# One block of the modulation sums moved from the key projection to the output projection

## The chip, the cores and the metric

The kernel runs on one core of one Trainium2 chip. A core has a matrix engine (TensorE, "PE" in the profile, its weight loads "PEld"), a vector engine (VectorE, "DVE"), a scalar engine (ScalarE, "ACT"), a general engine (GpSimd, "POOL") and a queue that issues the transfers (SyncE, "SP"). Each works through its own list of instructions in a fixed order and waits on semaphores for the others. The metric is the time of one execution on the device, in microseconds (us).

## The reference

One layer of a streaming encoder, for a sequence of 512 tokens and a width of 2048, all in float32:

```python
mod = c @ w_ada[l] + b_ada[l]
sh1, sc1, g1, sh2, sc2, g2 = [m[:, None, :] for m in jnp.split(mod, 6, axis=-1)]
h = x * (1.0 + sc1) + sh1
mix = token_mixer(h, ...)          # one input projection, three head groups, output projection w_o
x = layer_norm(ALPHA * x + g1 * mix, ln1_g[l], ln1_b[l])
h = x * (1.0 + sc2) + sh2
ff = jnp.square(jax.nn.relu(h @ w_ff1[l])) @ w_ff2[l]
x = layer_norm(ALPHA * x + g2 * ff, ln2_g[l], ln2_b[l])
```

The mixer projects h to the inputs of three groups: an S5 state-space scan with a gated linear unit, a gated convolution of width 3, and attention over 8 heads that keeps 128 keys per query, chosen by an indexer (scores, then a top-k mask). `c` is one vector, so `mod` is a product of a vector with a matrix of 2048 x 12288: some 100 MB of weights for very little arithmetic.

## The kernel before, in words

Matrix products run on TensorE in three passes: each weight tile is loaded as float32 (tile `raw`), split into a rounded part (`wh`, ScalarE, line 57) and the rest (`wl`, VectorE, line 60), and multiplied (lines 196 to 198 or 208 to 210). A quad is four k-tiles of 128 rows and 512 columns, 1 MB; `w_quads` loads one, steps the background queue, and splits it in two halves. `raw` has four buffers, which all loads of this kind share.

The modulation sums don't use TensorE for the product. `ada_acc` loads 1 MB (two rows of tiles of 128 x 1024) and adds each with VectorE to a running sum, weighted by an element of c per partition: `adaz <- raw * c + adaz` (line 63; the first of a block is a plain product, line 67, unless the sum starts from a bias row, when GpSimd clears the tile, line 220, and a small load, line 222, puts the bias into one row). A block is 1024 columns: 8 loads, 16 VectorE operations. Then a sink adds up over the partitions with small matmuls: `to_cols` (line 254) into a column of `mod2`, `to_rows` (line 246) into tiles `g1` that hold a gate for all rows. There is one buffer for `adaz`, so a block's first operation waits for the sink of the block before.

These blocks are generators in a list `bg`. `tick()` takes one step of the first of them: a load and its two sums; when a block is used up, the same step runs its sink and goes on to the first load of the next. `pump_tick()` is called once per quad and makes as many steps as `pump[0]` says, with fractions carried over. So `PUMP` sets how many loads go beside a quad of each stage.

The order of the stages in the program, with the quads of each: the first projections (indexer, query) in four groups of k-tiles; keys (8 quads), S5 (no quads), values (8 quads, rate 0), attention (none), convolution (three weight groups of 4 quads), output projection (16 quads in four column blocks `nb`), LayerNorm with the second modulation, MLP. The compiler's scheduler gives each engine its list: it takes the instruction of highest priority that is ready by its own estimate, in program order where priorities are equal. `prio(name)` raises it by an entry of `PRIO`: in the stages up to the convolution a weight split has 1000, a modulation sum 300, attention 600, S5 300, top-k 60, the indexer -100; in the output projection a split has 1500, its evictions 5000, a sum 150, and the loads of weights and sums 1500 each. The sinks' matmuls have none, so they keep their place among the program's matmuls.

Eight blocks belong to this change's surroundings: two for the gate g1 (`g1_jobs`) and four for the second shift and scale (`mod_jobs`: shift, scale, shift, scale, half of the width each). Two more, for the gate g2, come in the MLP and stay as they are. In the kernel before, three of `mod_jobs` are queued ahead of the keys; 16 steps there take the first two, the convolution's 12 steps take the third, and the output projection's 24 steps (1.5 per quad) and a few forced ones take gate block one, the fourth, gate block two. At the end of a column block the gate must be there: `while len(g1s) <= nb: tick()` forces steps until it is. After the projection four small operations finish `mod2`, and LayerNorm applies it while it transposes each row tile (`hf`).

Of the kernel before, what the change touches and what calls it, by code (L numbers as in the profile page):

```python
# [25 lines left out]
            wo=5000, ln1=150, ff1=3000, ff2=4000, hc=300, hc_load=300, tx=2000, ln2=150, index=-100, topk=60, rope=600, ssm0=600, ssm=300, glu=150,  # L26
            w_load0=4000, w_load1=300, w_load2=1500, w_load3=2500, w_split0=5000, w_split1=1000, w_split2=1500,
            w_split3=4000, ada_load0=4000, ada_load1=4000, ada_load2=1500, ada_load3=2500, ada0=5000, ada1=300,
            ada2=150, ada3=300)
PUMP = dict(start=0, keys=2, values=0, conv=1, wo=1.5)  # L30
BIG = 1e30
TWO_PI = 2.0 * math.pi
PI_LO = float(np.nextafter(np.float32(math.pi), np.float32(0)))
# [18 lines left out]
def trunk_kernel(ctx, tc, A, out):  # L52
# [3 lines left out]
    def act(o, i, f=AF.Copy, **kw):  # L56
        S.activation(o, i, f, **kw)  # L57

    def tt(o, a, b, op):
        V.tensor_tensor(o, a, b, op=op)  # L60

    def stt(o, a, s, b, op0, op1):
        V.scalar_tensor_tensor(o, a, s, b, op0=op0, op1=op1)  # L63
# [17 lines left out]
    def prio(name):  # L81
        if name not in PRIO:
            name += str(stage_no[0])
        return tc.high_priority(offset=PRIO[name])

    def bank(n="mm"):
        if "two" in pools:
            return two_banks()[:, 0]
        return pools[n].tile([128, 512], F32, name=n)
# [40 lines left out]
    def w_split(src, kk, n, pool=None, tag="w"):  # L130

        k2 = kk if pool else 2
        h = (pool or stage).tile([128, k2, n], F32R, name=tag + "h", bufs=3)[:, :kk]
        l = (pool or stage).tile([128, k2, n], F32R, name=tag + "l", bufs=3)[:, :kk]
        with prio("w_split"):
            split(h, l, src)
        return h, l

    def w_ks(dram, k0, k1, tick, pool, w=2):

        for a in range(k0, k1, w):
            b = min(a + w, k1)
            if w == 1:
                tick(a)
            r = load(dram[a:b].rearrange("k p n -> p k n"), [128, b - a, 512], pool, "rw")
            if w > 1:
                tick(b - a)
            h, l = w_split(r, b - a, 512)
            for j in range(a, b):
                yield j, h[:, j - a], l[:, j - a]  # L150

    bg = []

    def tick(n=1):

        for _ in range(n):
            while bg:
                try:
                    next(bg[0])
                    break  # L160
                except StopIteration:
                    bg.pop(0)

    pump, owed = [0], [0.0]
# [29 lines left out]
    def mm3(ps, wh, wl, xh, xl, start, stop):  # L194

        T.matmul(ps, wh, xh, start=start, stop=False)  # L196
        T.matmul(ps, wl, xh, start=False, stop=False)  # L197
        T.matmul(ps, wh, xl, start=False, stop=stop)  # L198
# [125 lines left out]
    def ensure(k):  # L324
        while ready[0] <= k:
            tick()
# [3 lines left out]
    mod_jobs = []  # L330
# [3 lines left out]
    for gi, (k0, k1) in enumerate(KGROUPS):  # L334
        n_ada = 2 * (KGROUPS[gi + 1][1] - KGROUPS[gi + 1][0]) if gi + 1 < len(KGROUPS) else PUMP["start"]
        n_w = 5 * (k1 - k0) - (k1 - k0 if gi == 0 else 0)
        done = [0, 0]

        def pace(n):
            done[0] += n  # L340
            want = min(-(-done[0] * n_ada // n_w), n_ada)
            tick(want - done[1])
            done[1] = want

        if gi > 0:
            ensure(k1 - 1)
        if gi == len(KGROUPS) - 1:
            bg.extend(mod_jobs[:3])

        first_k, last_k = k0, k1 - 1  # L350

        def evac_acc(dst, ps):
            with prio("kw"):
                if gi == 0:
                    act(dst, ps)
                else:
                    tt(dst, ps, dst, OP.add)


        banks = held[:2] + [bank() for _ in range(2)] + held[2:]  # L360
        if gi == 0:
            ws = w_ks(A["wA"], k0, k1, ensure, FP, 1)
        else:
            ws = w_ks(A["wA"], k0, k1, pace, FP)
        for k, h, l in ws:
            rb = FP.tile([128, 1, 80], F32, name="rkw")
            with prio("first"):
                nc.sync.dma_start(rb[:, 0], A["wkw"][k])
            hb, lb = w_split(rb, 1, 80, FP, "kw")
            for m in range(4):  # L370
                lim = (0, KT - 1) if m < 2 else (first_k, last_k)
                mm3(banks[m], h[:, m * 128:(m + 1) * 128], l[:, m * 128:(m + 1) * 128],
                    acts[:, k, 0], acts[:, k, 1], k == lim[0], k == lim[1])
            mm3(banks[4][:80], hb[:, 0], lb[:, 0], acts[:, k, 0], acts[:, k, 1], k == 0, k == KT - 1)
        for m in range(2, 4):
            evac_acc(u_t[:, m], banks[m])
        if last_k == KT - 1:
            with prio("kw"):
                act(kiwi[:80], held[2][:80])
                for m in range(2):  # L380
                    act(u_t[:, m], held[m])

        for b in range(2):
            banks = [bank() for _ in range(3)]
            for k, h, l in w_ks(A["wqi"][b], k0, k1, pace, FP):
                for t in range(3):
                    tk = slice((t + 1) * 128, (t + 2) * 128)
                    mm3n(banks[t], h, l, acts[:, k, 0, tk], acts[:, k, 1, tk], k == first_k, k == last_k)
            for t in range(3):
                evac_acc(qi_n[t][:, b * 512:(b + 1) * 512], banks[t])  # L390

        for b in range(2):
            banks = [bank() for _ in range(4)]
            for k, h, l in w_ks(A["wq"][b], k0, k1, pace, FP):
                for m in range(4):
                    mm3(banks[m], h[:, m * 128:(m + 1) * 128], l[:, m * 128:(m + 1) * 128],
                        acts[:, k, 0], acts[:, k, 1], k == first_k, k == last_k)
            for m in range(4):
                evac_acc(q_t[b][:, m], banks[m])
# [117 lines left out]
    def proj_t(dram, evac, quads=(0, 1, 2, 3), banks=None):  # L517
        banks = banks or [bank() for _ in range(4)]
        for i, (k, h, l) in enumerate(w_quads(dram, quads)):
            for m in range(4):  # L520
                mm3(banks[m], h[:, m * 128:(m + 1) * 128], l[:, m * 128:(m + 1) * 128],
                    acts[:, k, 0], acts[:, k, 1], i == 0, i == KT - 1)
        with prio("evac"):
            for m in range(4):
                evac(m, banks[m])
# [5 lines left out]

    pump[0] = PUMP["keys"]
    for b in range(2):
# [301 lines left out]
    VP = vp.enter_context(tc.tile_pool(name="vpool", bufs=3, reuse_waits="tile"))  # L835
    pump[0] = PUMP["values"]
    for b in range(2):
# [91 lines left out]

    pump[0] = PUMP["conv"]
    CV = mix.enter_context(tc.tile_pool(name="conv", bufs=1, reuse_waits="tile"))
    z_t = CV.tile([128, 4, SEQ], F32, name="z_t")
    proj_t(A["wconv"][0], lambda m, ps: act(z_t[:, m], ps))

    def conv_h(m, ps):
        tt(z_t[:, m], ps, z_t[:, m], OP.mult)
# [35 lines left out]
    wo = ExitStack()  # L974
# [4 lines left out]

    pump[0] = PUMP["wo"]  # L980
    stage_no[0] = 2
    g1_jobs = [ada_block(j, to_rows(g1_tile), True) for j in range(2)]
    bg.extend([g1_jobs[0], mod_jobs[3], g1_jobs[1]])
    xwh = WO.tile([128, 8, 512], F32R, name="xwh", bufs=1)
    xwl = WO.tile([128, 8, 512], F32R, name="xwl", bufs=1)
    for nb in range(4):
        banks = [bank() for _ in range(NT)]
        last = nb == 3

        def part(t, i, k, h, l):  # L990
            tk = slice(t * 128, (t + 1) * 128)
            mm3n(banks[t], h, l, acts[:, k, 0, tk], acts[:, k, 1, tk], i == 0, i == KT - 1)

        for i, w in enumerate(w_quads(A["wo"][nb], korder[:2] if last else korder)):
            for t in range(NT):
                part(t, i, *w)
        if last:
            ws = w_keep(A["wo"][nb], korder[2:], xwh, xwl)
            for t in range(NT):
                for i, w in enumerate(ws):  # L1000
                    part(t, 8 + i, *w)
        while len(g1s) <= nb:
            tick()
        for t in range(NT):
          with prio("wo"):
            o = r1[:, t, nb * 512:(nb + 1) * 512]
            xr = WO.tile([128, 512], F32, name="xr", bufs=2)
            nc.sync.dma_start(xr, A["x"][t * 128:(t + 1) * 128, nb * 512:(nb + 1) * 512])
            tt(o, banks[t], g1s[nb], OP.mult)
            stt(o, xr, ALPHA, o, OP.mult, OP.add)  # L1010
            V.bn_stats(out=stats[:, t, nb], in_=o)

    ts(mod2[:, 0], mod2[:, 0], 1.0, None, OP.add)
    tt(mod2[:, 3], mod2[:, 0], col("ln1b", 0, 16), OP.mult)
# [615 lines left out]
```

## Time and profile before

| | us |
|---|---|
| median of 3 runs | 2221.06 |
| range of the runs | 2219.15 to 2222.51 |
| the profiled execution: its time | 2218.12 |
| the profiled execution: its span, first to last instruction | 2216.3 |
| TensorE busy | 2138.7 (96%) |
| VectorE busy | 1878.6 (85%) |
| ScalarE busy | 1041.5 (47%) |
| sums into `adaz` (line 63), 180 operations | 198.2 |

Busy times are sums over the instructions of an engine; matmuls overlap in a pipeline, so a busy TensorE is not one at its peak. Idle time of an engine matters only where it is the one that the others wait for. Stretches are given in us from the first instruction; they follow the stages roughly: keys 250 to 340, values to 455, attention, S5 and convolution to 706, output projection to 877, LayerNorm to 925. The granted clock of TensorE is 0.993 of its full 2.4 GHz on the mean.

### The profile page before, as it was taken

The page shows a single profiled execution, that of the slowest core. Times are in us where ns is not written, and L with a number is a line of the kernel's source. Part 1 is how long each engine was busy: PE and PEld are TensorE (multiplying, and loading weights), DVE is VectorE, ACT ScalarE, POOL GpSimd, SP SyncE. Part 2 cuts the span into 40 slices and gives each one's busy share as a digit, 9 for nine tenths or more (in the row PEclk, how much of TensorE's full clock was granted, in tenths as well). Part 3 has the DMA queues.
Part 4 walks back from the last instruction along what each step waited for, and adds up shares of the span by engine and source line. Part 5 has one row for each costly group of instructions (what it writes and reads, how often), then busy time and mean ns, then how long its engine had stood idle before and what let it go on. Part 6 is the DMA issues. An engine that isn't in the chain of part 4 may idle for free.

```text
span 2216.3 us, 30985 instructions
## 1 busy us (share of the span) xinstructions
PE 2138.7 (96%) x12043; PEld 1845.9 (83%) x12043; DVE 1878.6 (85%) x2520; ACT 1041.5 (47%) x1394; POOL 44.6 (2%) x55
## 2 busy tenths in 40 slices
PE   6999999998999999989999999999899999999997
PEld 4778887876777787889999999999778887888886
DVE  7886799999867776798888888886789988998788
ACT  3423444344644313666666665665444444444432
POOL 0000000010000000000000000000000000000000
PEclk9999999999999999999999999999999999999999
DMA  8887653364334676756566556564888898798462
GB/s 326 316 305 280 200 216 135 107 235 164 103 119 157 243 277 255 241 172 229 182 205 203 188 198 206 181 209 141 301 295 275 280 318 280 245 341 275 134 218 86
DMA packets 198171, 489.80 MB, mean 221 GB/s; under 512 B 18052, under 2 KB 106500, under 8 KB 171656
## 3 DMA queue, kind: packets, MB, share of 16 engines
q1 hardware_dynamic: 191496, 475.24, 61.0%
q0 software_dynamic: 6528, 12.58, 3.1%
q8 instruction: 94, 1.54, 0.3%
q14 instruction: 53, 0.43, 0.1%
HBM read 394.45 MB, written 80.74 MB: 214 GB/s over the span
## 4 chain that ended last, share of the span: by engine, by line
PE 50%; issue 29%; DVE 14%; DMA 4%; ACT 3%; SPq 0%; POOL 0%; DVEq 0%; ACTq 0%; POOLq 0%
PE two L1396 7%; PE two L1397 7%; PE two L1395 7%; PE mm L209 4%; PE mm L197 4%; PE mm L210 4%; PE mm L208 3%; PE mm L198 3%; PE mm L196 3%; DVE wl L60 3%; DVE adaz L63 2%; PE two L210 1%; PE two L209 1%; PE two L208 1%; DVE x L60 1%
## 5 line engine op out<-in xcount | busy, mean ns | idle before, releaser
L57 ACT ACTIVATE wh<-raw 128x1024 fp32r<-128x1024 f32 x332 | 351.1, 1058 | 437.5 <-PE two L1397 140.8
L60 DVE TENSOR_TENSOR wl<-raw,wh 128x1024 fp32r<-128x1024 f32 x332 | 403.7, 1220 | 106.5 <-ACT wh L57 105.3
L1395 PE MATMUL two<-wh,hin 128*128 128x512 f32 x784 | 307.4, 392 | 5.7 <-ACT wh L57 5.0
L1396 PE MATMUL two<-wl,hin 128*128 128x512 f32 x784 | 306.5, 391 | 4.1 <-DVE wl L60 4.0
L1397 PE MATMUL two<-wh,hin 128*128 128x512 f32 x784 | 305.8, 390 | 0.0
L196 PE MATMUL mm<-acts,wh 128*128 128x512 f32 (+1 forms) x568 | 223.0, 396 | 5.7 <-ACT wh L57 3.3
L197 PE MATMUL mm<-acts,wl 128*128 128x512 f32 (+1 forms) x568 | 224.0, 394 | 1.7 <-DVE wl L60 1.5
L198 PE MATMUL mm<-acts,wh 128*128 128x512 f32 (+1 forms) x568 | 221.2, 391 | 0.0
L63 DVE SCALAR_TENSOR_TENSOR adaz<-raw,cols,adaz 128x1024 f32<-128x1024 f32 (+2 forms) x180 | 198.2, 1111 | 16.9 <-DMA raw<-in_adaR_dram 12.8
L202 PE MATMUL mm<-acts,wh 128*128 128x256 f32 x720 | 204.0, 283 | 3.1 <-ACT wh L57 2.4
L203 PE MATMUL mm<-acts,wl 128*128 128x256 f32 x720 | 203.8, 283 | 1.8 <-DVE wl L60 1.8
L203 PE MATMUL mm<-tx,wl 128*128 128x256 f32 x720 | 203.8, 283 | 1.1 <-DVE wl L60 1.1
L204 PE MATMUL mm<-acts,wh 128*128 128x256 f32 x720 | 203.7, 283 | 0.0
L204 PE MATMUL mm<-tx,wh 128*128 128x256 f32 x720 | 203.3, 282 | 0.0
L202 PE MATMUL mm<-tx,wh 128*128 128x256 f32 x720 | 202.0, 281 | 0.1
L1395 PEld LDWEIGHTS two<-wh,hin 128*128 128x128 f32 x784 | 147.7, 188 | 38.0 <-ACT wh L57 6.2
L1396 PEld LDWEIGHTS two<-wl,hin 128*128 128x128 f32 x784 | 147.6, 188 | 37.9 <-DVE wl L60 6.6
L209 PE MATMUL mm<-wl,acts 128*128 128x512 f32 x448 | 175.1, 391 | 1.7 <-DVE wl L60 1.5
L210 PE MATMUL mm<-wh,acts 128*128 128x512 f32 x448 | 174.5, 390 | 0.0
L208 PE MATMUL mm<-wh,acts 128*128 128x512 f32 x448 | 173.6, 391 | 0.2 <-DVE r L60 0.2
L1397 PEld LDWEIGHTS two<-wh,hin 128*128 128x128 f32 x784 | 147.6, 188 | 30.7
L57 ACT ACTIVATE wh<-st 128x1024 fp32r<-128x1024 f32 x90 | 95.5, 1061 | 105.3 <-PE mm L204 82.8
(316 smaller groups left out, 4514.5 us busy)
## 6 DMA issues: line engine op xcount, KB each, us to landing
raw<-in_wff_dram SPq DMA_DIRECT2D x232, 512.0 KB, 4.9
hc_d<-hc SPq DMA_DIRECT2D x98, 512.0 KB, 5.1
hin<-hc_d SPq DMA_DIRECT2D x49, 1024.0 KB, 9.2
raw<-in_adaR_dram SPq DMA_DIRECT2D x48, 1024.0 KB, 5.6
raw<-in_adaS_dram SPq DMA_DIRECT2D x32, 1024.0 KB, 9.0
raw<-in_wo_dram SPq DMA_DIRECT2D x16, 1024.0 KB, 5.3
araw<-in_adaR_dram SPq DMA_DIRECT2D x16, 1024.0 KB, 7.8
raw<-in_wconv_dram SPq DMA_DIRECT2D x12, 1024.0 KB, 5.0
```

Source lines behind the costliest of these rows:

```text
L57: S.activation(o, i, f, **kw)
L60: V.tensor_tensor(o, a, b, op=op)
L196: T.matmul(ps, wh, xh, start=start, stop=False)
L197: T.matmul(ps, wl, xh, start=False, stop=False)
L198: T.matmul(ps, wh, xl, start=False, stop=stop)
L202: T.matmul(ps, wh, xh, start=start, stop=False, skip_group_check=True)
L203: T.matmul(ps, wl, xh, start=False, stop=False, skip_group_check=True)
L204: T.matmul(ps, wh, xl, start=False, stop=stop, skip_group_check=True)
L209: T.matmul(ps, xh, wl, start=False, stop=False)
L1395: T.matmul(ps[:, t], xh, h[:, k], start=first, stop=False, skip_group_check=True)
L1396: T.matmul(ps[:, t], xh, l[:, k], start=False, stop=False, skip_group_check=True)
L1397: T.matmul(ps[:, t], xl, h[:, k], start=False, stop=last, skip_group_check=True)
```

## The change

Blocks of the modulation weights are handed out in another order and at other rates. Ahead of the keys two of `mod_jobs` are queued and not three, and the keys step the queue once per quad and not twice. The convolution still steps once per quad, but not in the first of its three weight groups. The output projection steps twice per quad, and its queue is: gate block one, the third of `mod_jobs`, gate block two, the fourth. A loop behind the projection empties the queue if anything is left.

```diff
-PUMP = dict(start=0, keys=2, values=0, conv=1, wo=1.5)
+PUMP = dict(start=0, keys=1, values=0, conv=1, wo=2)
...
         if gi == len(KGROUPS) - 1:
-            bg.extend(mod_jobs[:3])
+            bg.extend(mod_jobs[:2])
...
-    pump[0] = PUMP["conv"]
     CV = mix.enter_context(tc.tile_pool(name="conv", bufs=1, reuse_waits="tile"))
     z_t = CV.tile([128, 4, SEQ], F32, name="z_t")
     proj_t(A["wconv"][0], lambda m, ps: act(z_t[:, m], ps))
+
+    pump[0] = PUMP["conv"]
...
     g1_jobs = [ada_block(j, to_rows(g1_tile), True) for j in range(2)]
-    bg.extend([g1_jobs[0], mod_jobs[3], g1_jobs[1]])
+    bg.extend([g1_jobs[0], mod_jobs[2], g1_jobs[1], mod_jobs[3]])
...
             V.bn_stats(out=stats[:, t, nb], in_=o)
+    while bg:
+        tick()
```

## Rows read from the trace of the kernel before

**Rows 1.** Stretches (us from the start): engine busy us (instructions), granted clock, DMA share, GB/s

```profile
245.00:345.00 100.00, 99.58 (x463) 80.70 (x462) 93.71 (x130) 47.44 (x74) 0.00 (x0) 1.00 0.66 231
345.00:445.00 100.00, 99.27 (x436) 79.36 (x436) 97.60 (x203) 39.48 (x60) 1.29 (x3) 1.00 0.31 108
445.00:629.00 184.00, 166.27 (x920) 130.77 (x918) 171.85 (x545) 104.29 (x223) 9.70 (x16) 0.99 0.48 162
629.00:706.00 77.00, 76.78 (x334) 58.39 (x335) 49.24 (x66) 33.08 (x47) 0.95 (x1) 0.98 0.38 125
706.00:757.00 51.00, 49.77 (x223) 40.16 (x222) 36.59 (x41) 18.14 (x26) 0.00 (x0) 1.00 0.64 235
757.00:799.00 42.00, 41.75 (x184) 34.08 (x183) 35.17 (x36) 7.91 (x8) 0.00 (x0) 1.00 0.79 294
799.00:847.00 48.00, 48.00 (x221) 40.04 (x220) 38.47 (x41) 8.37 (x8) 0.95 (x1) 1.00 0.74 282
833.00:877.00 44.00, 43.31 (x188) 34.85 (x187) 30.28 (x33) 12.19 (x13) 0.00 (x0) 1.00 0.74 281
```

**Rows 2.** The same view for instructions on the tile adaz: PE, PEld, DVE, POOL

```profile
245.00:345.00 100.00, 1.90 (x16) 2.02 (x16) 25.03 (x20) 0.00 (x0) 1.00 0.66 231
...
445.00:629.00 184.00, 1.84 (x16) 1.94 (x16) 19.96 (x16) 0.00 (x0) 0.99 0.48 162
629.00:706.00 77.00, 1.84 (x16) 1.94 (x16) 7.68 (x6) 0.95 (x1) 0.98 0.38 125
706.00:757.00 51.00, 1.54 (x3) 0.68 (x4) 12.79 (x10) 0.00 (x0) 1.00 0.64 235
...
833.00:877.00 44.00, 2.15 (x4) 0.68 (x4) 10.23 (x8) 0.00 (x0) 1.00 0.74 281
```

**Rows 3.** TensorE's waits from 445 to 640 us: total, times, longest

```profile
PE sa L891 <- ACT s L57: 4.9, 8, 2.6
PE sb L719 <- DVE s L60: 3.8, 4, 2.6
PE mm L196 <- ACT ve L57: 2.3, 2, 1.2
PE sa L543 <- DVE sqa L60: 2.2, 1, 2.2
PE sa L899 <- DVE st L881: 1.4, 2, 1.1
PE sa L891 <- DVE st L881: 1.1, 1, 1.1
```

**Rows 4.** Timeline of VectorE, 303 to 338 us: start, duration, line, operation

```profile
304.90 0.75 DVE L67 TENSOR_SCALAR adaz<-raw,cols 128x1024 f32<-128x1024 f32 x1
...
306.17 1.28 DVE L63 SCALAR_TENSOR_TENSOR adaz<-raw,cols,adaz 128x1024 f32<-128x1024 f32 x1
```

**Rows 5.** Timeline of the SP queue, 455 to 465 us

```profile
455.79 4.18 SPq L847 DMA_DIRECT2D v_d<-ve  x4
...
461.73 0.32 SPq L868 DMA_DIRECT2D qh<-q_d  x1
```

**Rows 6.** Timeline of VectorE in the output projection, with idle time before

```profile
781.02 1.23 DVE L60 TENSOR_TENSOR wl<-raw,wh 128x1024 fp32r<-128x1024 f32 x1 [0.94 <-ACT wh L57]
782.16 2.60 DVE L63 SCALAR_TENSOR_TENSOR adaz<-raw,cols,adaz 128x1024 f32<-128x1024 f32 x2
786.46 1.23 DVE L60 TENSOR_TENSOR wl<-raw,wh 128x1024 fp32r<-128x1024 f32 x1 [1.70 <-ACT wh L57]
```

**Rows 7.** Timeline of GpSimd, 640 to 830 us

```profile
648.54 0.95 POOL L220 MEMSET adaz<- 128x1024 f32 x1 [50.53 <-PE sc L254]
```

**Rows 8.** Timeline of TensorE at the end of the first column block

```profile
754.69 1.02 PE L246 MATMUL sc<-adaz,ones 128*128 128x512 f32 x2
```

**Rows 9.** Timeline of ScalarE in LayerNorm

```profile
883.01 0.46 ACT L57 ACTIVATE hf<-sa,mod 128x128 f32<-128x128 f32 x1 [0.75 <-PE sa L1044]
```

## Prediction

> **What bounds the kernel now.** I read three views in this order: the busy time of each engine by stretch [rows 1], the same for the tile `adaz` alone, which holds the sums over the modulation weights [rows 2], and TensorE's waits where the first view shows it idle [rows 3]. In the first the reader is to compare two columns. From 245 to 445 us TensorE is busy 99.58 and 99.27 of each 100 us and VectorE 93.71 and 97.60 [rows 1]: both are full, TensorE with the key and value projections, VectorE with the indexer, the key rotation and the top-k. From 445 to 629 us TensorE is busy 166.27 of 184 us, so it loses 17.7, and VectorE is at 171.85, or 93% [rows 1]: attention, the S5 scan and the gated convolution share it. From 629 us on TensorE is full again, 76.78 of 77, 49.77 of 51, 41.75 of 42, 48.00 of 48 [rows 1], while VectorE has 49.24 of 77 there and 72% to 84% of each stretch of the output projection up to 847 us [rows 1]. So the projection is bound by TensorE and has slack on VectorE; ahead of it lies a stretch in which VectorE hardly pauses and TensorE waits.
>
> The waits tell whose fault that is: from 445 to 640 us TensorE waits 3.8, 2.2, 1.4 and 1.1 us for VectorE, 8.5 in all, but also 4.9 us for ScalarE's softmax tile and 2.3 us for ScalarE's eviction of the values [rows 3]. About half of the loss is VectorE's; the other half belongs to attention's own step from scores to softmax to transpose, and to the start of the convolution.
>
> **Part 1, the keys.** At a rate of 1 instead of 2 the eight weight quads of the keys step the queue 8 times and not 16: one block and not two is summed there. A block is 8 loads of 1 MB and 16 VectorE operations, the first 0.75 us, the others 1.28 [rows 4]: 0.75 + 15 x 1.28 = 20.0 us. Of the two blocks, 20 operations (25.03 us) stand between 245 and 345 us [rows 2]; the other 12 lie before. Of the one block that stays, spread over eight quads, I expect half in that stretch, 8 operations. So 12 fewer: 15.4 us off a queue whose gaps are 6.3 us in that stretch and 2.4 in the next 100 [rows 1]. The top-k, which follows in the same queue, should end 10 to 15 us sooner. TensorE gains nothing there, since it is full.
>
> **Part 2, the convolution.** Still one block, but stepped in the last two of the three weight groups. The 16 operations (19.96 us) that stand between 445 and 629 us [rows 2] now come some quads later; I count 3 of them past 629, where VectorE has 27.8 us free [rows 1]: 3.8 us. In all 15.4 + 3.8 = 19 us leave VectorE's queue ahead of 629 us.
>
> What is that worth to TensorE? At most all of its 17.7 us. At the other end nothing or a small loss: attention cannot start sooner, since its first query load is issued at 461.73 us, right behind the store of the values, which hang on TensorE's own value projection [rows 5]; and a sum that now comes ahead of a late head's softmax step costs that step up to 1.28 us, so I put that end at a loss of 3. Between -17.7 and +3 I take the part that VectorE releases, 8.5 us of the list: **-9 us**. Once that stall is gone the next one is the wait for ScalarE's softmax, which stays.
>
> **Part 3, the output projection.** It now steps 32 times, two per quad. The order is: sink of the convolution's block and gate block one, shift, gate block two, scale, each sink in the step that starts the next block; one forced step after the first column block makes 33, which is what 4 x 8 loads and the last sink need. Gate block one is out where it was; gate block two ends in the last quad of the third column block, the scale's in the last of the fourth. The loop added at the end finds nothing to do. 24 loads become 32; with 16 weight quads that is 3 raw tiles per quad for 4 buffers.
>
> VectorE can take that rate: around 780 us each half quad of 5.44 us already holds one split (1.23) and one load's two sums (2.60) with a gap of 1.70 us [rows 6]. Two loads per quad fit, and four quads leave 8 x 1.70 = 13.6 us for evictions. This cover is thin at two places.
>
> First column block. The gate's sums need the only `adaz` buffer. Before, the sink ahead of them let GpSimd clear the tile at 648.54 us [rows 7], and 6 operations (7.68 us) were done by 706 us [rows 2]. Now that sink runs with the projection's first quad, at about 708 us; the clear (0.95 us) and the bias row's load follow. Behind that load SP's queue holds the next raw tiles, and ScalarE's split and then TensorE wait for those. All 16 operations fall behind some 711 us, and TensorE takes them up at 754.69 us [rows 8]. VectorE's 36.59 us from 706 to 757 [rows 1] grow by the six, 7.7, to 44.3 of 51. It fits with little to spare: **+1 us**; ends 0 and 7.7, the six wholly exposed.
>
> Fourth column block. The scale's block is new here. From 833 to 877 us VectorE had 30.28 us [rows 1], of which 10.23 are the gate's sums that now come sooner [rows 2]: 20.05 + 20.0 = 40 of 44 us. The first activation that needs the result starts at 883.01 us [rows 9]. So there is room, but the sums, the last two weight quads and the MLP's first weights share four buffers, and the LayerNorm behind them has few matmuls to hide anything: **+2 us**; ends 0 and 20, the whole block.
>
> Against that, gate block two no longer ends on forced steps after the third column block, and the 0.69 us that TensorE loses from 833 to 877 us [rows 1] can go: **-1 us** (0 to -1). The MLP's first weights arrive some loads later and wait for LayerNorm in any case; the matmuls of the sinks, the clears and all other loads are moved, not added: 0.
>
> **Sum:** -9 + 1 + 2 - 1 = -7 us on the profiled execution, which took 2218.12 us for a span of 2216.3: 2211. The median of the runs, 2221.06, lies 2.9 above it; carried over, **2214 us**.
>
> **Rivals.** *Attention keeps its own pace (B).* Each head is a chain through ScalarE, ranked ahead of the scan on VectorE, and the first starts at 461.73 us whatever the top-k does [rows 5]. For it: the longest entry of the waits, 4.9 us, is ScalarE's [rows 3]. Against it: with VectorE at 93%, attention's own steps queue there too. Gain 2, cost 2: 2221 us.
>
> *The fourth column block overflows (C), slower.* The scale's sums come last in the rotation of the raw tiles. If they find none of the gaps, their 20.0 us run on behind 877 us; 6.0 are free until 883.01 [rows 9], so the scale behind LayerNorm comes 14 us late, and everything after it. The rival decides from the point where the last sum ends later than 881 us, 883.01 less 1.84 for the sink's matmuls [rows 2]. With a gain of 4 ahead of it: 2221 + 14 - 4 = 2231 us. For it: 40 of 44 us leaves no room for a bad order. Against it: the gap of 1.70 us in every half quad [rows 6]. The Trainium skill (Perfetto Trace Analysis, section Identifying Performance Opportunities) says that a gap repeating on the engine that should be saturated can mean too few buffers for the next tile; by that rule three tiles per quad in four buffers would show as equal gaps on TensorE in all four column blocks, and the time would be this rival's or worse. The rows of the kernel before, at 2.5 tiles per quad, show no such gap there.
>
> *All of the loss goes (D).* VectorE delays ScalarE's steps as well, and every wait of the list shrinks: -17.7 + 2 = -16, 2205 us.
>
> **Chances.** My forecast (A, own range 2207 to 2218) 0.46, B 0.27, C 0.19, D 0.08. A measurement tells 0.2%, or 4.4 us, from no change: faster is below 2216.6, slower above 2225.5. Faster: A but for its upper end (0.41), D, and 0.03 of B, 0.52. Slower: C and the upper tail of B, 0.23. The rest, 0.25, is same. The range goes from D's 2205 to just under C's 2231, so about a tenth is left out on either side.
>
> **What would show it.** Right: the top-k ends near 430 us, TensorE's loss from 445 to 629 us falls from 17.7 to about 9, the projection's first matmul moves from 706 to near 697 us, and from there to LayerNorm it takes 2 us more than before. Wrong in parts 1 and 2: the top-k ends sooner and TensorE loses as much as before (B). Wrong in part 3: TensorE waits for a weight split in the fourth column block, or ScalarE's first `hf` waits for `mod2` (C). The whole is wrong if VectorE's sums in the projection take fewer than 64 operations.

## The result and the profile after: slower by 0.74%

The changed kernel takes 2236.78 us (median of 4 runs, 2234.98 to 2240.29), the kernel before 2221.52 on the same chip (4 runs, 2219.15 to 2222.51): 1.0074 times as long, 95% interval 1.0059 to 1.0089 (the quotient of the two medians is 1.0069; here and below a ratio is taken over the single runs). The prediction had the sign wrong, and the time lies above its range. The profiled execution has a span of 2234.6 us against 2216.3, 18.3 more, and the rest of this section says where these stand.

The stretches of [rows 1], in the kernel after, with the one behind them added (columns: stretch, its length, busy us and instructions of PE, PEld, DVE, ACT, POOL, granted clock, DMA share, GB/s):

```profile
245.00:345.00 100.00, 97.93 (x449) 78.55 (x448) 92.35 (x147) 52.55 (x85) 0.00 (x0) 1.00 0.52 179
345.00:445.00 100.00, 97.62 (x427) 78.17 (x426) 96.42 (x219) 37.23 (x52) 3.06 (x6) 1.00 0.30 102
445.00:629.00 184.00, 165.22 (x935) 132.03 (x934) 164.39 (x506) 104.65 (x227) 7.88 (x12) 0.98 0.44 141
629.00:706.00 77.00, 76.94 (x316) 57.68 (x316) 44.76 (x54) 31.57 (x41) 0.00 (x0) 1.00 0.43 154
706.00:757.00 51.00, 50.75 (x237) 41.63 (x235) 42.64 (x47) 16.94 (x25) 0.95 (x1) 1.00 0.72 268
757.00:799.00 42.00, 41.57 (x189) 34.37 (x190) 35.22 (x36) 8.66 (x10) 0.95 (x1) 1.00 0.74 274
833.00:877.00 44.00, 44.00 (x191) 35.59 (x190) 36.50 (x37) 9.36 (x10) 0.00 (x0) 1.00 0.82 311
877.00:925.00 48.00, 39.23 (x218) 33.52 (x216) 32.36 (x74) 29.38 (x51) 0.00 (x0) 0.86 0.75 261
```

VectorE did get its relief: 7.5 us less from 445 to 629 us than in [rows 1]. TensorE's idle time there did not fall; it is 18.8 us against 17.7, and from 245 to 445 us it is 4.45 against 1.15. In the projection TensorE is full, 44.00 of 44 us in the last column block. The loss opens in the last line: 8.8 of 48 us idle at a granted clock of 0.86. The same stretch in the kernel before:

```profile
877.00:925.00 48.00, 43.75 (x283) 39.31 (x282) 33.56 (x74) 32.98 (x59) 0.00 (x0) 0.96 0.64 213
```

The sums stand where the change puts them. The same view for the tile `adaz` alone (PE, PEld, DVE, POOL), to be held against [rows 2]:

```profile
245.00:345.00 100.00, 0.00 (x0) 0.00 (x0) 12.80 (x10) 0.00 (x0) 1.00 0.52 179
...
706.00:757.00 51.00, 2.87 (x18) 2.32 (x18) 20.43 (x16) 0.95 (x1) 1.00 0.72 268
833.00:877.00 44.00, 2.08 (x4) 0.68 (x4) 19.97 (x16) 0.00 (x0) 1.00 0.82 311
877.00:925.00 48.00, 1.95 (x16) 1.86 (x16) 2.57 (x2) 0.00 (x0) 0.86 0.75 261
```

Two of the scale's operations and its sink stand behind 877 us. What this does is seen in VectorE's list at the end of the projection, first in the kernel before (start, duration, line, operation, and in brackets the idle time ahead and what ended it):

```profile
876.97 0.69 DVE L60 TENSOR_TENSOR r<-mm,g 128x512 f32<-128x512 f32 x1 [3.12 <-PE mm L210]
...
878.42 0.69 DVE L1011 BATCH_NORM_STATS2 stats<-r 128x6 f32<-128x512 f32 x1
879.15 0.27 DVE L1019 BATCH_NORM_AGGREGATE mv<-stats 128x2 f32<-128x24 f32 x1
```

and then in the kernel after:

```profile
877.77 2.60 DVE L63 SCALAR_TENSOR_TENSOR adaz<-raw,cols,adaz 128x1024 f32<-128x1024 f32 x2 [0.53 <-DMA raw<-in_adaR_dram]
880.29 0.68 DVE L60 TENSOR_TENSOR r<-mm,g 128x512 f32<-128x512 f32 x1
882.42 0.17 DVE L60 TENSOR_TENSOR mod<-sc,cols 128x8 f32<-128x8 f32 x1 [1.44 <-PE sc L254]
...
883.11 0.17 DVE L67 TENSOR_SCALAR mod<-mod 128x16 f32<-128x16 f32 x1
883.23 0.69 DVE L1012 BATCH_NORM_STATS2 stats<-r 128x6 f32<-128x512 f32 x1
885.56 0.69 DVE L60 TENSOR_TENSOR r<-mm,g 128x512 f32<-128x512 f32 x1 [1.64 <-PE mm L210]
886.17 1.22 DVE L60 TENSOR_TENSOR wl<-raw,wh 128x1024 fp32r<-128x1024 f32 x1
...
887.90 1.22 DVE L60 TENSOR_TENSOR wl<-raw,wh 128x1024 fp32r<-128x1024 f32 x1
...
889.64 1.21 DVE L60 TENSOR_TENSOR wl<-raw,wh 128x1024 fp32r<-128x1024 f32 x1
890.77 0.26 DVE L1022 BATCH_NORM_AGGREGATE mv<-stats 128x2 f32<-128x24 f32 x1
```

The first row tile of the projection is ready at about the same time in both (its last pass begins at 871.3 and 870.9 us), and the first `r` in each list is its eviction. The reader is to follow three steps. The eviction and the row statistics stand behind the last two sums and behind `mod`, which waits for the sink: `stats` starts 4.81 us later (878.42 to 883.23). `mv` is the first of LayerNorm's scalars. Between the statistics and `mv` three splits of the MLP's first weights (`wl`, 3.4 us from start to start), the eviction and statistics of the next row tile (1.8) and a wait of 1.64 us for that tile's matmuls have come in: another 6.81 us (`mv` 879.15 to 890.77, 11.62 in all). From `mv` to the first `hf` it takes 2.13 us more: ScalarE now normalizes two row tiles in a row before it, where it did one. ScalarE's list, its second line to be held against [rows 9]:

```profile
892.77 4.09 ACT L57 ACTIVATE r<-r,mv 128x2048 f32<-128x2048 f32 x2 [0.31 <-DVE mv L63]
896.76 0.44 ACT L57 ACTIVATE hf<-sa,mod 128x128 f32<-128x128 f32 x1
```

That is 13.75 us later. From there the MLP's first matmul (line 202) starts 69.8 us behind the first `hf`, against 69.5 before. The MLP's first stage, from its first to its last matmul of that line, takes 614.5 us against 611.0, and what follows 653.5 against 652.8. The view of that line, before and after (first and last start):

```profile
L202 PE MATMUL mm<-acts,wh x720: 278/283/386, 952.5 to 1563.5; 128*128 128x256 f32 x180
```

```profile
L202 PE MATMUL mm<-acts,wh x720: 274/283/415, 966.6 to 1581.1; 128*128 128x256 f32 x180
```

So 13.75 + 0.3 + 3.5 + 0.7 = 18.3 us, the whole difference of the spans.

### The profile page after: what moved, and what is told of

Its sections match the earlier page's. It is cut to its first block, busy times and chain, and to the rows that moved or that the text cites. A ratio compares the mean times of both kernels' runs of the same rounds, so it can differ in the third digit from the quotient of the medians.

```text
span 2234.6 us, 31017 instructions
## 1 busy us (share of the span) xinstructions
PE 2147.8 (96%) x12043; PEld 1854.7 (83%) x12043; DVE 1882.0 (84%) x2520; ACT 1043.2 (47%) x1394; POOL 44.6 (2%) x55
## 3 DMA queue, kind: packets, MB, share of 16 engines
q8 instruction: 94, 1.54, 0.3%
## 4 chain that ended last, share of the span: by engine, by line
PE 72%; DVE 18%; DMA 5%; ACT 2%; issue 2%; SPq 0%; DVEq 0%; POOL 0%; ACTq 0%; POOLq 0%
PE mm L203 8%; PE mm L202 8%; PE mm L204 8%; PE two L1399 5%; PE two L1400 5%; PE two L1398 5%; DVE wl L60 4%; PE mm L210 4%; PE mm L208 4%; PE mm L209 4%; PE mm L197 4%; PE mm L198 4%; PE mm L196 4%; DVE ffa L60 2%; DVE adaz L63 2%
## 5 line engine op out<-in xcount | busy, mean ns | idle before, releaser
L202 PEld LDWEIGHTS mm<-acts,wh 128*128 128x128 f32 x720 | 139.9, 194 | 6.2 <-ACT ev L57 3.3
```

Of the source, the lines that this page charges most:

```text
L202: T.matmul(ps, wh, xh, start=start, stop=False, skip_group_check=True)
```

## The experiments

Ratios are against the kernel before on the same chip, times are medians; the milestones come from one profiled execution of each. The columns: the top-k's end as the start of S5 behind it (line 603, VectorE), attention's last matmul (line 543), TensorE's idle time from 245 to 706 us, LayerNorm's first `hf`, the length of the MLP's first stage. In run 10 the first two lines are 605 and 545. A milestone of a single execution is not exact: run 8, whose program ahead of LayerNorm is that of the kernel before, reaches the projection 4.6 us later than it.

| kernel | ratio, 95% interval | top-k | attention | idle | first `hf` | stage |
|---|---|---|---|---|---|---|
| before | 1 | 443.7 | 629.2 | 19.1 | 883.0 | 611.0 |
| after | 1.0074, 1.0059 to 1.0089 | 432.4 | 604.6 | 23.3 | 896.8 | 614.5 |
| 1 no fourth block | 0.9983, 0.9972 to 0.9995 | 435.0 | 607.8 | 23.4 | 885.7 | 610.9 |
| 2 keys alone | 0.9998, 0.9987 to 1.0009 | 430.5 | 603.4 | 22.1 | 883.6 | 612.4 |
| 3 projection alone | 1.0057, 1.0038 to 1.0076 | 445.5 | 614.3 | 20.9 | 895.5 | 617.2 |
| 4 LayerNorm ranked first | 1.0029, 1.0017 to 1.0041 | 433.1 | 606.1 | 21.5 | 891.8 | 611.7 |
| 5 nothing ahead | 1.0018, 1.0009 to 1.0027 | 424.8 | 603.9 | 24.6 | 890.5 | 614.2 |
| 6 rate 2.5 | 1.0084, 1.0068 to 1.0101 | 433.6 | 605.7 | 22.0 | 903.4 | 612.2 |
| 7 rate 2.5, LayerNorm first | 1.0088, 1.0070 to 1.0106 | 429.6 | 602.8 | 22.6 | 898.9 | 611.5 |
| 8 rank alone, before | 1.0012, 1.0002 to 1.0022 | 447.7 | 633.7 | 18.4 | 887.6 | 611.7 |
| 9 six loads | 1.0034, 1.0017 to 1.0051 | 432.4 | 605.2 | 21.7 | 888.9 | 618.1 |
| 10 six transfers | 1.0039, 1.0024 to 1.0054 | 430.7 | 603.3 | 22.3 | 890.3 | 612.8 |

**The first four** take the change apart. Theory at that point: the relief ahead of the projection buys TensorE nothing, and the fourth block makes LayerNorm late.

**1, the change without its fourth block.**

```diff
-    bg.extend([g1_jobs[0], mod_jobs[2], g1_jobs[1], mod_jobs[3]])
+    bg.extend([g1_jobs[0], mod_jobs[2], g1_jobs[1]])
+    G.memset(mod2[:, 0, 8:16], 0.5)
```

> The changed kernel without its fourth block in the output projection: the second half of the MLP's scale is a constant 0.5, and its 8 loads, 16 sums and sink are left out; the order and rates are otherwise those of the changed kernel. Theory L (the block that ends last in the fourth column block holds LayerNorm back, and the relief beside the keys is worth nothing to TensorE): the first LayerNorm activation that needs the scale comes back from 897 us to 883 to 886 us, time 2217 to 2223 us, the same as before. Rival G (the relief does give its 9 us, and the projection alone loses 24): 2208 to 2214 us. Rival R (the rate of two loads per quad, or the convolution's later steps, cost the time): 2230 us or more.

Measured: 2221.03 us, 0.9983. The whole loss hangs on this block, but with all of the relief and 20 us of sums less the kernel gains only 0.2%.

**2, the relief alone**: three blocks ahead as before, the second and third spread later.

```diff
-PUMP = dict(start=0, keys=2, values=0, conv=1, wo=1.5)
+PUMP = dict(start=0, keys=1, values=0, conv=2, wo=1.5)
...
-    pump[0] = PUMP["conv"]
...
+    pump[0] = PUMP["conv"]
...
+    while bg:
+        tick()
```

> One block beside the keys as in the changed kernel, but the block that leaves them goes to the convolution, two loads per quad in its last two weight groups; the output projection has its three blocks at 1.5 per quad as before. Theory L: TensorE's idle time from 245 us to the projection stays at 19 to 23 us and the projection ends as before, so 2217 to 2226 us. Rival G: VectorE's relief from 245 to 445 us is worth its 9 us: 2210 to 2214 us. If the convolution's raw buffers are the trouble, over 2230 us.

Measured: 2223.43 us, 0.9998. The top-k ends 13 us sooner and attention 26, and the projection's first matmul comes at 710.09 us against 708.35: the relief reaches attention and stops there.

**3, the fourth block alone**: two blocks beside the keys at the old rate, none beside the convolution, four beside the projection.

```diff
-PUMP = dict(start=0, keys=2, values=0, conv=1, wo=1.5)
+PUMP = dict(start=0, keys=2, values=0, conv=0, wo=2)
...
-            bg.extend(mod_jobs[:3])
+            bg.extend(mod_jobs[:2])
...
-    bg.extend([g1_jobs[0], mod_jobs[3], g1_jobs[1]])
+    bg.extend([g1_jobs[0], mod_jobs[2], g1_jobs[1], mod_jobs[3]])
```

> Two blocks beside the keys as before; the block of the convolution goes to the output projection, which has the four blocks, order and rate of the changed kernel; the convolution has no sums. Theory L: the late LayerNorm comes with the projection's four blocks, whatever stands ahead: its first scaled activation 11 to 15 us later than the end of the first row tile allows, 2232 to 2240 us. Rival A (the changed kernel loses because attention and the convolution were reordered ahead of the projection): 2216 to 2224 us.

Measured: 2239.1 us, 1.0057, first `hf` at 895.50, 12.5 us late where the change has 13.75, with the keys untouched.

**4, the change with LayerNorm's work ranked above the MLP's weight splits.**

```diff
-            wo=5000, ln1=150, ff1=3000, ...
+            wo=5000, ln1=6000, ff1=3000, ...
```

> The changed kernel with LayerNorm's priority raised from 150 to 6000, so that its scalars stand in VectorE's and ScalarE's lists ahead of the MLP's first weight splits. Theory L1 (LayerNorm is late by its place in the lists; the last sums are out at 881 us, only 3 us late): first scaled activation at 885 to 889 us, not 897, time 2222 to 2229 us. Theory L2 (LayerNorm waits for the sums themselves, whatever the order): 2234 to 2239 us, as the changed kernel.

Measured: 2230.74 us, 1.0029, first `hf` at 891.77: both lie between the two theories' ranges, nearer to L1's. VectorE's list in this kernel:

```profile
879.23 2.60 DVE L63 SCALAR_TENSOR_TENSOR adaz<-raw,cols,adaz 128x1024 f32<-128x1024 f32 x2
881.75 0.68 DVE L60 TENSOR_TENSOR r<-mm,g 128x512 f32<-128x512 f32 x1
883.91 0.17 DVE L60 TENSOR_TENSOR mod<-sc,cols 128x8 f32<-128x8 f32 x1 [1.48 <-PE sc L254]
...
884.72 0.69 DVE L1012 BATCH_NORM_STATS2 stats<-r 128x6 f32<-128x512 f32 x1
...
886.26 0.26 DVE L1022 BATCH_NORM_AGGREGATE mv<-stats 128x2 f32<-128x24 f32 x1
```

The splits are gone from between the statistics and `mv` (886.26 against 890.77, although the sums end 1.5 us later here), the wait for the sink is still there. So the two steps read from the list are separate costs: from `stats` to `mv` it now takes 1.54 us, 0.81 more than before and not 6.81. By the ratios some 10 of the change's 16.4 us (0.0074 x 2222) go with the rank. Not all of them are the order of the list: the first `hf` comes 5.0 us sooner than in the change, and the MLP's first stage is 2.8 us shorter. Nor is all that stays due to the late sums. The four operations that finish `mod2` have no rank, here as before; the last of them starts at 891.51 us, behind three splits, 0.26 us ahead of the first `hf`.

**5, nothing ahead of the projection**, the strongest relief that there is.

```diff
-PUMP = dict(start=0, keys=2, values=0, conv=1, wo=1.5)
+PUMP = dict(start=0, keys=0, values=0, conv=0, wo=1.5)
...
-            bg.extend(mod_jobs[:3])
+            G.memset(mod2[:, 0:2], 0.5)
```

> The kernel before without the three blocks of sums that stand ahead of the output projection (shift's first half, scale's first half, shift's second half): 24 loads of 1 MB and 48 VectorE operations, some 60 us of VectorE, are left out and these columns are set to 0.5. The projection keeps its own three blocks. Theory now (TensorE's idle time beside attention is attention's own pace, and relief of VectorE there buys nothing): 2217 to 2223 us, TensorE idle 15 to 19 of the 184 us from 445 to 629 us, projection's first matmul at 704 to 709 us. Rival (the step of the prediction: half of that idle time is VectorE's, worth 8.5 us, and the change failed to collect it for another reason): 2212 us or less, TensorE's idle time there at most 10 us.

Measured: 2227.24 us, 1.0018: not a gain but a small loss, and the projection's first matmul at 714.48 us. The stretch of attention in this kernel:

```profile
445.00:629.00 184.00, 163.24 (x906) 128.59 (x906) 149.62 (x448) 107.45 (x227) 6.97 (x9) 0.97 0.37 118
```

VectorE has 22 us less than in [rows 1] and TensorE is idle for 20.8 of 184 us. The theory said 15 to 19, and the prediction's step at most 10. Attention ends at 603.9 us here, at 604.6 in the change and at 603.4 in run 2, with very different work beside it. It is not that attention starts sooner: its first query load is issued at 468.21 us in the change, against 461.73 [rows 5]. It runs faster, and with fewer other matmuls beside it. The first pass of the projections' matmuls (line 196, which the convolution uses here) from 445 to 605 us, in the kernel before, in the kernel after and in run 5 (shortest, median and longest of them in ns, first and last start):

```profile
L196 PE MATMUL mm<-acts,wh x103: 387/389/792, 453.7 to 605.0; 128*128 128x512 f32 x103
```

```profile
L196 PE MATMUL mm<-acts,wh x71: 387/397/796, 454.8 to 603.5; 128*128 128x512 f32 x71
```

```profile
L196 PE MATMUL mm<-acts,wh x63: 387/396/791, 474.5 to 605.0; 128*128 128x512 f32 x63
```

From 605 to 706 us there are 87, 118 and 118. What used to fill attention's pauses runs behind it instead, and the projection begins no sooner.

**6 and 7, a rate of 2.5 in the projection**, so that the scale's block would end sooner, 7 with LayerNorm's rank as well.

```diff
-PUMP = dict(start=0, keys=1, values=0, conv=1, wo=2)
+PUMP = dict(start=0, keys=1, values=0, conv=1, wo=2.5)
```

> The changed kernel with 2.5 steps per quad in the output projection and not 2, so that its four blocks end some three quads before its end. Theory now (the loss is the scale's late sink, which sets when LayerNorm starts): the last sum ends by 868 us, the first hf starts at 880 to 886 us, 2218 to 2225 us. Rival (the loss is the fourth block's load on the stretch, 20 us of VectorE and 8 MB, wherever it stands in it): 2232 us or more, with TensorE's waits for weight splits in the third column block instead.

> The same rate of 2.5, and LayerNorm's work ranked at 6000 and not 150, above the MLP's weight splits. Theory now: with the sums early LayerNorm is not queued behind MLP splits in any case, so the rank adds nothing, 2217 to 2224 us and within 2 us of the run with the rate alone; first hf 879 to 884 us. Rival (the splits ahead of LayerNorm are a loss of their own whenever the fourth block stands there): 4 us or more below the run with the rate alone.

Measured: 2242.90 us, 1.0084, and 2242.72, 1.0088 (interval 1.0070 to 1.0106). The expected repair failed. The sums did not end early, the last at 877.96 us, because the projection itself became slower: its last pass over the first row tile begins at 891.7 us and not 870.9. TensorE's longest entry of waits from 757 to 877 us (total, times, longest) is

```profile
PE mm L209 <- DVE wl L60: 9.1, 3, 3.0
```

The three stand at the starts of the second, third and fourth column block (763.92, 815.65 and 867.31 us). What leads up to the middle one, from the lists of VectorE (DVE) and TensorE (PE):

```profile
773.71 10.52 DVE L63 SCALAR_TENSOR_TENSOR adaz<-raw,cols,adaz 128x1024 f32<-128x1024 f32 x8
...
794.23 0.17 DVE L60 TENSOR_TENSOR mod<-sc,cols 128x8 f32<-128x8 f32 x1 [4.62 <-PE sc L254]
...
809.35 2.73 DVE L60 TENSOR_TENSOR r<-mm,g 128x512 f32<-128x512 f32 x4 [2.26 <-PE mm L210]
...
814.39 1.21 DVE L60 TENSOR_TENSOR wl<-raw,wh 128x1024 fp32r<-128x1024 f32 x1
...
815.65 0.50 PE L209 MATMUL mm<-wl,acts 128*128 128x512 f32 x1 [3.02 <-DVE wl L60]
```

Eight sums in a row and two more end a block; then VectorE waits 4.62 us for the sink, which stands in TensorE's list among the projection's matmuls. SP's queue issues no transfer from 784.6 to 795.24 us, since the next one, the bias row of gate block two, waits for `adaz` to be cleared, and that for the sink. The third column block's first weights are issued at 799.89 us, ScalarE has them at 809.43, their split stands behind the evictions, and TensorE waits 3.02 us. TensorE itself has no gap while VectorE waits for the sink. The list was read at this one place, and none of its links was tried alone. So these runs say nothing of an early scale; they show only that a rate of 2.5 is no repair. The rank is worth nothing in them (0.2 us between the medians), as expected, since LayerNorm's `mv` follows its row tile by the usual 7.9 us.

**8, the rank in the kernel before**, a control for run 4 (its edit, made in the kernel before).

> The kernel before with LayerNorm's work ranked at 6000 and not 150, nothing else changed. Control for the run of the changed kernel with that rank, which took off 6 us. Theory now (the rank repairs only what the late sums push behind the splits): 2217 to 2225 us, first hf within 2 us of 883. Rival (the rank is worth the same in any kernel): 2214 to 2217 us, first hf at 878 to 880 us.

Measured: 2225.43 us, 1.0012. The rank has no gain of its own; `mv` follows the row tile by 7.8 us in both. The first `hf` comes 4.6 us later than in the kernel before because this execution reaches the projection 4.6 us later (712.94). Run 4's gain is thus a repair of what the late sums push behind the splits.

**9 and 10, the change with two loads less in the scale's block**: 9 leaves out the loads and their four operations, 10 the loads alone.

```diff
...
-        src = [A["adaR"][blk][:, 2 * j:2 * j + 2] for j in range(8)]
+        src = [A["adaR"][blk][:, 2 * j:2 * j + 2] for j in range(6 if short else 8)]
...
```

> The changed kernel with the last two of the eight loads of the block in the fourth column block left out (2 MB and 4 VectorE operations, 5.1 us; that half of the scale lacks them). It separates when the sums end from how much is summed: three quarters of the block stay on the same stretch. Lateness (VectorE's list is held up by the last two loads and the sink behind them): last sum done by 875 us, LayerNorm's first scalar operation at 879 to 883 us, first hf at 883 to 888 us, 2219 to 2226 us. Load (each operation of the block costs its share wherever it stands): a quarter of the loss comes back, 2232 to 2236 us, first hf at 892 to 895 us.

> The changed kernel with all 16 operations of that block, but the last two loads left out: their four operations read the tile that is already there (that half of the scale is wrong by it). It takes 2 MB off the transfers and leaves VectorE's work. If the last sums are late because their tiles arrive late (issued at 869.78 us, ready at 877.77): they end 3 to 6 us sooner, first hf at 884 to 890 us, 2221 to 2229 us. If VectorE itself is too full by then: last sum done at 878 us or later, first hf at 893 us or later, 2232 to 2238 us.

Measured: 2232.29 us, 1.0034, and 2232.96, 1.0039 (interval 1.0024 to 1.0054); the kernel before took 2225.76 on their chip. VectorE's list in run 9:

```profile
869.32 2.60 DVE L63 SCALAR_TENSOR_TENSOR adaz<-raw,cols,adaz 128x1024 f32<-128x1024 f32 x2
873.96 0.17 DVE L60 TENSOR_TENSOR mod<-sc,cols 128x8 f32<-128x8 f32 x1 [2.04 <-PE sc L254]
...
881.16 0.69 DVE L60 TENSOR_TENSOR r<-mm,g 128x512 f32<-128x512 f32 x1 [1.77 <-PE mm L210]
...
882.49 1.22 DVE L60 TENSOR_TENSOR wl<-raw,wh 128x1024 fp32r<-128x1024 f32 x1
883.63 0.69 DVE L1012 BATCH_NORM_STATS2 stats<-r 128x6 f32<-128x512 f32 x1
884.35 0.26 DVE L1022 BATCH_NORM_AGGREGATE mv<-stats 128x2 f32<-128x24 f32 x1
```

A quarter of the block gone brings back 7.9 of the 13.75 us of the first `hf` (888.85 us). A cost per operation would have brought back a quarter, 3.4; so the end of the block, 8.5 us sooner here (871.92), counts for more than its size, though this run changes both. The time came out above the range that lateness was given, and the first `hf` just above its: LayerNorm is 5.8 us later than before, 2.5 of it because the projection's last pass comes that much later, and the MLP's first stage takes 618.1 us, 7.1 more, at a low clock (last section). Run 10 is inconclusive on its own question. Without the two loads the scheduler laid the list out anew, with the last sums singly between the evictions and ending at 883.42 us, so it doesn't tell late transfers from a full VectorE. `mv` comes at 883.93 us there and the first `hf` at 890.30.

No version here beats the kernel before with all of the work done; run 2 equals it.

## Why the prediction was wrong

**What bounds the kernel, and part 1.** Right as far as it went. The top-k was to end near 430 us and ends at 432.4. The 12 sums fewer from 245 to 345 us are 10 (12.80 us stay, against 25.03).

**Part 2, -9 us: this step failed first.** It priced the relief by the waits that name VectorE, 8.5 us [rows 3], and took it that they would go. In the kernel after, the longest entries of the same view are

```profile
PE sb L719 <- DVE s L60: 7.5, 4, 6.3
PE sa L891 <- ACT s L57: 6.0, 9, 1.3
PE sa L899 <- DVE st L881: 2.1, 2, 1.7
PE sa L878 <- DVE st L881: 1.3, 1, 1.3
```

The entries with VectorE did not shrink in sum, though VectorE had more room. With one of 0.4 us below these lines they come to 11.3 us, against 9.2 before (the 8.5 and one of 0.7 below [rows 3]). S5's `s` went from 3.8 to 7.5, ScalarE's softmax from 4.9 to 6.0. A wait that names an engine says who came last, not that this engine was short of time. The run that takes 60 us off VectorE (5) and the run that moves the relief alone (2) agree: worth 0 to TensorE, within what can be measured. That is rival B's result for this part, and its reason held in part: attention does not start sooner. But it does not keep its own pace either, as B had it. It ends 25 us sooner, and the convolution's matmuls move from beside it to behind it (103 to 71 passes).

**Part 3, first column block, +1, and gate block two, -1.** Both were small, as said. The ten sums there became 16 (20.43 us), VectorE went from 36.59 to 42.64 of 51 us (44.3 forecast), and TensorE lost less than before, 0.25 us against 1.23; the 0.69 us from 833 to 877 us is gone. The projection starts 1.65 us later, at 710.00 us, and its last matmul is at 897.56 us against 897.71. (The prediction's signs gave 706 us for that start in the kernel before; it is 708.35.)

**Part 3, fourth column block, +2: this step failed by most.** Busy time came out close, 36.50 of 44 us where 40 was worked out, and there was room left over. But room was the wrong question. The load of the block's last tile is issued at 869.78 us, VectorE still waits for it until 877.77, its sums end at 880.37, and they stand ahead of the evictions in VectorE's list. The prediction did name rival C, with 14 us for the late `hf` and 2231 us; the delay is 13.75. That the two agree is luck: C's 14 was all 16 sums running on behind 877 us, and only two did. Its condition was off too: it asked for a last sum later than 881 us, and 880.37 was enough, since LayerNorm waits not only for the scale but for everything that stands behind the sums and the sink in that list, and for the MLP splits that then came first. Runs 1, 3, 4 and 9 show this in turn: without the block, with the block alone, with the splits out of the way, with its end cut off. With nothing gained ahead and 13.75 + 3.5 lost, the time lies above rival C's 2231, which had credited 4 us of gain.

The Trainium skill's rule on repeating gaps (Perfetto Trace Analysis, section Identifying Performance Opportunities) was weighed in the prediction as a case against this part. The equal gaps that the prediction took from it did not come at three tiles per quad: TensorE is busy 50.75 of 51, 41.57 of 42 and 44.00 of 44 us. They did come at 3.5 (run 6), three of 3.0 us, one at the start of each later column block. Whether a lack of buffers makes them was not tried.

**The sum.** Forecast -7; measured, in the profiled spans, +18.3: part 2 gave 0 for -9, the fourth column block 13.75 for +2, the MLP's first stage 3.5 for 0, and 1.0 stands between and behind these.

## What to carry to other kernels

Before taking work off an engine to relieve a wait, ask whether the work that fills the wait would only move: take all of the work off once, and see if the bound engine's idle time falls. When background work is moved to the end of a stage, look not at the free time there but at which instructions of the next stage stand behind its last operation in the same list, and what the scheduler will put ahead of them once they are late. A block whose last two sums ended some 3 us behind the stage cost 13.75 here, and the stage that followed 3.5 more.

## What the runs showed of the hardware

TensorE's clock took a share that I had priced at nothing. In the kernel after, behind the scale's sink (sixteen one-column matmuls, 880.43 to 882.38 us), the projection's matmuls of 512 columns start 0.43 us apart until 885.7 us and 0.23 from then on; the granted clock from 880 to 890 us is 0.83, the mean of a stretch at the upper level, 2.4 GHz, and some at the lower, 1.2. A sink of the same sixteen stands at 812.37 us in the kernel before with the clock at 1.00 throughout [rows 1], so the sink alone doesn't do it. Behind LayerNorm the length of the MLP's first stage goes with the clock. Its rows from 960 to 1010 us, in the kernel before, in the kernel after and in run 9:

```profile
960.00:1010.00 50.00, 44.66 (x363) 43.66 (x363) 44.32 (x50) 28.67 (x39) 0.00 (x0) 1.00 0.69 234
```

```profile
960.00:1010.00 50.00, 42.07 (x293) 39.92 (x292) 44.05 (x46) 26.80 (x40) 0.00 (x0) 0.90 0.49 163
```

```profile
960.00:1010.00 50.00, 45.10 (x311) 43.90 (x310) 40.67 (x43) 25.59 (x35) 0.00 (x0) 0.83 0.47 158
```

The stage takes 611.0, 614.5 and 618.1 us in these three. Over all twelve kernels it goes with that clock: 610.9 and 611.0 at 1.00, 611.5 to 612.8 in six kernels at 0.97 and 0.93, 614.2 and 614.5 at 0.90, 617.2 and 618.1 at 0.83. TensorE pauses in this stretch in the kernel before as well (44.66 of 50 us busy) and keeps the full clock. Its longest pause from 945 to 1015 us is 1.8 us there, 2.9 in the kernel after and 3.4 in run 9; but run 5 falls to 0.90 with none above 1.7. What makes the difference between such pauses was not tried and stays open.
